# One visit per head for the 32-column products of a recurrent layer, and four output-projection tiles whose last quarter runs late

## The chip, the cores and the metric

The kernel runs on one core of a Trainium2 chip. The metric is device time in microseconds (us) of one execution. The engines are PE (matrix products; it writes PSUM), DVE (vector), ACT (scalar), POOL and SP (here: the queue that issues most DMAs).

## The reference

One inference step of two layers: layer 0 is a gated linear recurrence (HGRN2), layer 1 sliding-window attention. 272 prompt tokens (16 learned ones ahead of 256) and 64 sample tokens (8 sequences of 8) go through the same weights. Model width is 2048, layer 0 has 16 heads of 128.

```
h = x @ w_in;  q, f, i, g = split(h)          # 4 x 2048 columns
f = lb + (1 - lb) * sigmoid(f);  k = 1 - f;  v = i
per head, over time:   S <- diag(f) S + k v^T;   o = q S
o = rmsnorm(o) * norm_w * silu(g)
x <- LayerNorm(alpha * x + o @ w_out)          # then layer 1
```

The states S of the prompt and of each sample sequence are outputs too.

## The kernel before

Everything is kept transposed: channels on partitions, 336 tokens along the free axis. Weights and activations are split into a high and a low part, so that one projection product is three PE products (lines 225 to 227) with 336 columns each.

A class `Stream` (line 108) sets the order of the work. Its list `seq` names weight chunks of 4 x 128 rows; a projection tile (128 output columns) has four chunks. `run` (line 195) loads the raw weights 14 chunks ahead (`raw`, in pairs of chunks, into the pool `wraw` of four buffers, line 254), converts them 4 to 7 chunks ahead (`conv_hi` on ACT, line 159; `conv` on DVE, line 170) and issues the products. After each three products it calls `step`, which lets up to two of the side generators run (line 179). A generator says with `yield n` after how many steps it wants to go on. So a tile is 16 steps, and the yields lay every other instruction of the layer between the projections; each engine executes its own instructions in the order in which they are issued. A generator that yields too early makes PE wait, and all projections behind it.

Layer 0 runs four tiles per head in the order f, q, i, g. For each head `head_chain` (line 502) starts after tile q:

- `update` scales k and q with running products of f, at distances 1, 2, 4 (first), then 8, 16, 32, 64. The results lie in the tiles `kx`, `qx`, of which there is one set for all heads.
- First visit (lines 547 to 551): 88 products of 32 columns for the tile `lv_a` (`level`), one quarter of the array each; then, by `adv`, the tail of the head before: `psp` (three products for the prompt's state), `pss` (two for the sample states), and the three transposes of `osc` of the head before that.
- `pick` copies the wanted places of `lv_a` into a mask-selected tile `a32` (tile `a` in the profile).
- Second visit (lines 585 to 606): `lv_b` (34 products of 32 columns), `po` of the head before (28 products of 32 columns, 6 of 128), and six transposes into `pk` and `pv`.
- Behind it `at` is written from `lv_b`, `V`, `K`, `Ks`, `Vs` are copied from `pk` and `pv` in a row (lines 619 to 634), and `vm` is made on POOL.

`head_tail` (line 654) is a generator advanced by hand with `adv`: state products, their eviction and the stores of the states, `po`, the squares and `osc` (normalisation, lines 706 to 715), its transposes, and the gate with `sg`, whose result `oh`, `ol` the output projection reads. `sg` is made from tile g: a sigmoid on ACT at once, a product with PSUM on DVE two steps later (line 457).

PSUM: three banks `pj` for projection tiles, two banks `lv`, three banks `mm` for the rest. The output projection (tiles z0 to z15, line 811) needs `oh` of all heads: chunk kc reads heads 4kc to 4kc+3. So that the last heads have time, z0, z1, z2 run their chunks in turn (`kouter`, line 812). When z0 is done, the side work is drained, the pools of layer 0 are closed, and `z_chain` (line 785) evicts each z tile.

Of the kernel before, what the change touches and what calls it, by code (L numbers as in the profile page):

```python
# [21 lines left out]
F32 = mybir.dt.float32  # L22
# [7 lines left out]
P = 128  # L30
# [8 lines left out]
H = 16  # L39
# [200 lines left out]
def hybrid_trunk(tc, x_prompt, x_sample, state_hgrn, cache_k, cache_v, meta, w_in0, lb_logits, norm_w, w_out0,  # L240
# [7 lines left out]
    with es:  # L248
# [86 lines left out]
        vecs = ct("vecs", [P, P])  # L335
# [14 lines left out]
        kx, qx = [], []  # L350
        for q in range(1, 4):
            for l, nm, w in ((kx, "kx", 384), (qx, "qx", 448)):
                l.append(hp1.tile([P, w], F32, tag=f"{nm}{q}", name=f"{nm}{q}"))
                nc.gpsimd.memset(l[-1], 0.0)
# [90 lines left out]
        def epi_g(h):  # L445
            def epi(ps):
                d = head_state(h)
                sg = hp.tile([P, T], F32, tag="sg", name=f"sg{h}")
                nc.scalar.activation(sg, ps, AF.Sigmoid)
                d["sg"] = sg  # L450
                s0 = hp.tile([P, 8, P], F32, tag="s0", name=f"s0_{h}")
                nc.sync.dma_start(s0, state_hgrn[0, :, h].rearrange("b k v -> k b v"))
                d["s0"] = s0

                def chain():
                    yield 2
                    nc.vector.tensor_tensor(sg, sg, ps, op=ALU.mult)  # L457
                    ready["g", h] = True
                st.spawn(chain())
            return epi  # L460
# [5 lines left out]
        def update(k, q, m, tot, n, k2=None, q2=None, nq=None):  # L466
# [5 lines left out]
            w = min(n, 448 - (m - 1)) // (2 * m) * 2 * m  # L472
# [4 lines left out]
            if q2 is not None and not nq:  # L477
                nc.scalar.copy(halves(q2, m - 1, m, w, True), halves(q, m - 1, m, w, True))
# [4 lines left out]
        def total(h, m, tot, n):  # L483
            nb = n // (2 * m)
            o = hp.tile([P, nb], F32, tag=f"tot{2 * m}", name=f"tot{h}_{2 * m}")
# [10 lines left out]
        tails = {}  # L496

        def adv(h):
            if h in tails:
                next(tails[h], None)  # L500

        def head_chain(h):
            d = head_state(h)
            kr, qp, a32, sq, qi = d["kr"], d["qp"], d["a32"], d["sq"], d["qi"]
            at = d["at"].rearrange("p (b w) -> p b w", b=3)
            kk = [kr] + kx
            qq = [qp] + qx

            def level(pl, o, li, wide=True):
                k, q = kk[min(li, 3)], qq[min(li, 3)]  # L510
                for blk in range(3):
                    for j in range(4 if blk < 2 else 3 if wide else 1):
                        c = blk * 128 + j * 32
                        nc.tensor.matmul(pl[32 * j:32 * j + 32, o + blk * 32:o + blk * 32 + 32], k[:, c:c + 32],
                                         q[:, c:c + 32], start=True, stop=True, tile_position=(0, 32 * j),
                                         skip_group_check=True)

            def pick(pl, o, li, wide=True):
                m0 = li * 96
                r = 96 if wide else 32  # L520
                nc.vector.copy_predicated(a32[:, 0:64], mk[:, m0:m0 + 64], pl[:, o:o + 64])
                nc.vector.copy_predicated(a32[0:r, 64:96], mk[0:r, m0 + 64:m0 + 96], pl[0:r, o + 64:o + 96])

            tot = {1: d["f"]}
            yield 3
            for li in range(3):
                m = 1 << li
                update(kk[li], qq[li], m, tot[m], 352, kk[li + 1], qq[li + 1])
                tot[2 * m] = total(h, m, tot[m], 352)
                yield 4  # L530

            k8, q8 = kk[3], qq[3]
            fs = hp.tile([P, 8], F32, tag="fs", name=f"fs{h}")
            t8 = tot[8]
            nc.gpsimd.tensor_copy(fs, t8[:, 36:44])
            w64 = d["w64"]
            nc.gpsimd.tensor_copy(w64[:, 0:64].rearrange("p (b t) -> p b t", t=8)[:, :, 7], fs)

            for s in range(3):
                n = 3 if s < 2 else 2  # L540
                nc.gpsimd.tensor_tensor(sq[:, 0:96 * n].rearrange("p (j w) -> p j w", w=96)[:, :, 40 * s:40 * s + 8],
                                        q8[:, 288:288 + 24 * n].rearrange("p (j w) -> p j w", w=24)[:, :, 8 * s:8 * s + 8],
                                        w64[:, 0:24 * n].rearrange("p (j w) -> p j w", w=24)[:, :, 8 * s:8 * s + 8],
                                        op=ALU.mult)
            yield 4

            pa = lv.tile([P, 512], F32, tag="lv", name=f"lv{h}_a")
            for li in range(4):
                level(pa, 96 * li, li)
            adv(h - 1)  # L550
            adv(h - 2)
            yield 1
            update(k8, q8, 8, t8, 272)
            tot[16] = hp.tile([P, 17], F32, tag="tot16", name=f"tot{h}_16")
            t8v = t8[:, 0:34].rearrange("p (b two) -> p b two", two=2)
            nc.vector.tensor_tensor(tot[16], t8v[:, :, 0], t8v[:, :, 1], op=ALU.mult)
            for li in range(4):
                pick(pa, 96 * li, li)
            adv(h - 1)
            yield 2  # L560
            t16 = tot[16][:, 16:17]
            update(k8, q8, 16, tot[16], 256, kk[1], qq[1])
            tot[32] = total(h, 16, tot[16], 256)
            nc.vector.tensor_scalar(qq[1][:, 271:272], q8[:, 271:272], t16, None, op0=ALU.mult)
            yield 3
            adv(h - 2)
            update(kk[1], qq[1], 32, tot[32], 256, kk[2], qq[2])
            nc.scalar.copy(qi[:, 144:161], qq[1][:, 255:272])
            t64 = total(h, 32, tot[32], 256)
            t128 = hp.tile([P, 2], F32, tag="t128", name=f"t128_{h}")  # L570
            nc.vector.tensor_tensor(t128[:, 0:1], t64[:, 2:3], t64[:, 3:4], op=ALU.mult)
            yield 3
            adv(h - 1)
            k64 = kk[2]
            nc.vector.tensor_tensor(halves(kr, 0, 64, 256), halves(k64, 0, 64, 256),
                                    t64.rearrange("p (b two) -> p b two", two=2)[:, :, 1:2].to_broadcast([P, 2, 64]),
                                    op=ALU.mult)
            nc.scalar.copy(halves(kr, 0, 64, 256, True), halves(k64, 0, 64, 256, True))
            nc.vector.tensor_scalar(qi[:, 64:128], qq[2][:, 191:255], t64[:, 2:3], None, op0=ALU.mult)
            nc.scalar.copy(qi[:, 0:64], qq[2][:, 127:191])  # L580
            yield 5
            while ("i", h) not in ready:
                yield 0

            pb = lv.tile([P, 512], F32, tag="lv", name=f"lv{h}_b")
            d["pb"] = pb
            level(pb, 0, 4, wide=False)
# [11 lines left out]
            adv(h - 1)  # L599
            iT = d["iT"]  # L600
            pk = pm(f"pk{h}")
            for j in range(3):
                nc.tensor.transpose(pk[:, j * P:(j + 1) * P], (kr if j < 2 else k8)[:, j * P:(j + 1) * P], ident)
            pv = pm(f"pv{h}")
            for j in range(3):
                nc.tensor.transpose(pv[:, j * P:(j + 1) * P], iT[:, j * P:(j + 1) * P], ident)
            yield 1
            pick(pb, 0, 4, wide=False)
            for a in range(2):
                nc.scalar.copy(at[64 * a:64 * a + 32, 0:2, 64 * a + 32:64 * a + 64],  # L610
                               pb[64 * a:64 * a + 32, 96:160].rearrange("p (b w) -> p b w", b=2))
            nc.scalar.copy(at[0:64, 0:2, 64:128], pb[0:64, 160:288].rearrange("p (b w) -> p b w", b=2))
            for blk in range(3):
                o = 1 if blk < 2 else 0
                nc.vector.copy_predicated(
                    at[:, blk, o:o + 128].rearrange("p (j w) -> p j w", w=32),
                    mk[:, 480 + blk * 128:608 + blk * 128].rearrange("p (j w) -> p j w", w=32),
                    a32[:, blk * 32:blk * 32 + 32].unsqueeze(1).to_broadcast([P, 4, 32]))
# [29 lines left out]
            for w, us in ((1, (h - 1,)), (3, (h - 1,)), (6, (h,)), (2, (h - 1, h)), (1, (h - 1, h)), (4, (h,)), (3, (h,)),  # L648
                          (2, (h,)), (4, (h,)), (1, (h,))):
                yield w  # L650
                for u in us:
                    adv(u)
# [849 lines left out]
```

## Time and profile before

| | us |
|---|---|
| median of 3 runs (lowest, highest) | 1155.41 (1155.01, 1156.36) |
| the profiled execution | 1155.55 |
| its span from first to last instruction | 1153.5 |
| PE busy in the span | 1138.6 (99%) |
| DVE, ACT, POOL busy | 795.3, 619.8, 238.8 |

The 16 heads of layer 0 take from about 9 to 574 us, the output projection to about 702 us, layer 1 the rest. Lines of the timeline read: start in us, duration, engine, line of the kernel, operation, tile written <- tiles read, shapes, how many instructions are merged in the row, and in brackets the idle time ahead of it with what ended it. The durations of PE are modelled, its starts are measured. A transposition is a PE product too.

### The profile page before, as it was taken

Reading aid. Unit: us, or ns where it says so; the run is one execution under the profiler, and the core shown is the slowest. Engines: PE = TensorE matmul, PEld = TensorE weight load, DVE = VectorE, ACT = ScalarE, POOL = GpSimd, SP = SyncE. Lnnn points to the kernel's source line nnn. Section 1 sums busy time; section 2 is a strip of 40 time slices with the busy share of each in tenths; the row PEclk is TensorE's granted clock in tenths of the full one; section 3 lists DMA queues with packets and bytes.
Section 4 is the critical chain, followed back from the end, with each engine's and each line's share of the span. In section 5 each row is a group of like instructions: output and inputs, shape, how many; then the busy total and the mean of one; then the engine's idle time right before and its main releaser. Section 6 shows DMA issues by size and latency. Waiting matters only on the chain.

```text
span 1153.5 us, 26363 instructions
## 1 busy us (share of the span) xinstructions
PE 1138.6 (99%) x10151; PEld 1105.6 (96%) x10151; DVE 795.3 (69%) x2094; ACT 619.8 (54%) x1771; POOL 238.8 (21%) x343
## 2 busy tenths in 40 slices
PE   9999999999999999999999999999999999999996
PEld 9999999999999999999999999998999999999995
DVE  4766566666576565666678777577878767787657
ACT  4664555545555545555445445566666655555540
POOL 2121221212212112212134332100000011145510
PEclk9999999999999999999999999999999999999998
DMA  9654565445554545654455545653533535545572
GB/s 255 190 148 132 165 178 144 133 141 168 165 155 144 149 132 165 182 145 134 135 169 146 147 143 140 199 143 106 137 106 106 147 101 166 146 134 159 155 211 91
DMA packets 322877, 173.39 MB, mean 150 GB/s; under 512 B 19104, under 2 KB 317536, under 8 KB 322720
## 3 DMA queue, kind: packets, MB, share of 16 engines
q1 hardware_dynamic: 320656, 166.98, 51.4%
q0 software_dynamic: 1344, 4.20, 1.3%
q8 instruction: 80, 1.31, 0.5%
q10 hardware_dynamic: 752, 0.52, 0.1%
q14 instruction: 45, 0.37, 0.1%
HBM read 158.88 MB, written 14.42 MB: 150 GB/s over the span
## 4 chain that ended last, share of the span: by engine, by line
PE 94%; DVE 3%; ACT 1%; DMA 0%; issue 0%; SPq 0%; POOL 0%; DVEq 0%
PE pj_g L225 7%; PE pj_g L226 7%; PE pj_g L227 7%; PE pj_q L225 6%; PE pj_q L226 6%; PE pj_q L227 6%; PE pj_f L225 3%; PE pj_i L225 3%; PE pj_f L226 3%; PE pj_f L227 3%; PE pj_i L227 3%; PE pj_i L226 3%; PE pj_z L225 3%; PE pj_z L227 3%; PE pj_z L226 3%; PE pj_y L225 2%
## 5 line engine op out<-in xcount | busy, mean ns | idle before, releaser
L225 PE MATMUL pj_g<-xh,wlo_g 128*128 128x336 f32 (+1 forms) x512 | 163.1, 319 | 0.0
L225 PE MATMUL pj_q<-xh,wlo_q 128*128 128x336 f32 (+1 forms) x512 | 163.0, 318 | 0.0
L226 PE MATMUL pj_g<-xl,whi_g 128*128 128x336 f32 (+1 forms) x512 | 160.8, 314 | 0.0
L226 PE MATMUL pj_q<-xl,whi_q 128*128 128x336 f32 (+1 forms) x512 | 160.8, 314 | 0.0
L227 PE MATMUL pj_g<-xh,whi_g 128*128 128x336 f32 (+1 forms) x512 | 160.6, 314 | 0.0
L227 PE MATMUL pj_q<-xh,whi_q 128*128 128x336 f32 (+1 forms) x512 | 160.4, 313 | 0.0
L225 PEld LDWEIGHTS pj_q<-xh,wlo_q 128*128 128x128 f32 x512 | 96.8, 189 | 0.7
L225 PEld LDWEIGHTS pj_g<-xh,wlo_g 128*128 128x128 f32 x512 | 96.8, 189 | 0.3
L226 PEld LDWEIGHTS pj_g<-xl,whi_g 128*128 128x128 f32 x512 | 97.0, 189 | 0.0
L226 PEld LDWEIGHTS pj_q<-xl,whi_q 128*128 128x128 f32 x512 | 96.9, 189 | 0.0
L227 PEld LDWEIGHTS pj_q<-xh,whi_q 128*128 128x128 f32 x512 | 96.7, 189 | 0.0
L227 PEld LDWEIGHTS pj_g<-xh,whi_g 128*128 128x128 f32 x512 | 96.6, 189 | 0.0
L170 DVE TENSOR_TENSOR wlo_g<-raw_g,whi_g 128x512 fp32r<-128x512 f32 x128 | 91.8, 752 | 0.1
L159 ACT CAST whi_g<-raw_g 128x512 fp32r<-128x512 f32 x128 | 76.4, 622 | 21.6 <-DMA raw_g<-in_hgrn_w_in_dram 13.0
L170 DVE TENSOR_TENSOR wlo_q<-raw_q,whi_q 128x512 fp32r<-128x512 f32 x128 | 85.2, 685 | 2.5 <-ACT whi_q L159 2.5
L636 POOL TENSOR_TENSOR vm<-Vs,cst 96x512 fp32r<-96x512 f32 x32 | 33.7, 1055 | 252.4 <-DVE Vs L633 251.3
L225 PE MATMUL pj_f<-xh,wlo_f 128*128 128x336 f32 x256 | 83.2, 325 | 0.0
L225 PE MATMUL pj_z<-oh,wlo_z 128*128 128x336 f32 x256 | 81.5, 318 | 1.2 <-DVE sg L457 1.2
L225 PE MATMUL pj_i<-xh,wlo_i 128*128 128x336 f32 x256 | 81.5, 318 | 0.0
L226 PE MATMUL pj_f<-xl,whi_f 128*128 128x336 f32 x256 | 81.3, 318 | 0.0
L227 PE MATMUL pj_z<-oh,whi_z 128*128 128x336 f32 x256 | 81.3, 317 | 0.0
L227 PE MATMUL pj_f<-xh,whi_f 128*128 128x336 f32 x256 | 81.1, 317 | 0.0
(404 smaller groups left out, 3217.4 us busy)
## 6 DMA issues: line engine op xcount, KB each, us to landing
raw_z<-in_hgrn_w_out_dram SPq DMA_DIRECT2D x32, 512.0 KB
raw_q<-in_swa_w_in_dram SPq DMA_DIRECT2D x32, 512.0 KB
raw_g<-in_swa_w_in_dram SPq DMA_DIRECT2D x32, 512.0 KB
raw_f<-in_hgrn_w_in_dram SPq DMA_DIRECT2D x30, 512.0 KB
raw_q<-in_hgrn_w_in_dram SPq DMA_DIRECT2D x30, 512.0 KB
raw_i<-in_hgrn_w_in_dram SPq DMA_DIRECT2D x30, 512.0 KB
raw_g<-in_hgrn_w_in_dram SPq DMA_DIRECT2D x30, 512.0 KB
raw_y<-in_swa_w_out_dram SPq DMA_DIRECT2D x24, 512.0 KB
```

Source lines behind the costliest of these rows:

```text
L159: e.nc.scalar.copy(hi, t["raw", kc])
L170: e.nc.vector.tensor_tensor(lo, t.pop(("raw", kc)), hi.bitcast(F32), op=ALU.subtract)
L225: nc.tensor.matmul(ps, lo[:, kk, :], xh, start=first, stop=False)
L226: nc.tensor.matmul(ps, hi[:, kk, :], xl, start=False, stop=False)
L227: nc.tensor.matmul(ps, hi[:, kk, :], xh, start=False, stop=last)
L636: nc.gpsimd.tensor_tensor(vm[0:96, 4 * u:4 * u + 4, :], Vs[:, u, :].bitcast(F32).unsqueeze(1).to_broadcast([96, 4, P]), cst[0:96, 0:4].uns ...
```

## The change

1. Each head has one visit for 32-column products. `visit0(h)` issues `lv_a` of head h, then `lv_b` of head h-1 (`wide_levels`), `po` of head h-2 (`output`) and the transposes `pk`, `pv` of head h-1. After the last head two more visits finish the pipeline. A visit waits, in the order of issue, until `due(h)` says that what it reads has been issued.
2. `kx` and `qx` exist twice, by the parity of the head. `qp` and `qx` are 384 columns wide instead of 448; `sg` has three buffers, `sp` two. `nmb` and `rbc` move from the constants into a pool opened when layer 0's pools close, and `vecs` shares the buffer of `ns`.
3. `states(h)` holds what `head_tail` did for the states, as a generator of its own with its own yields: the copies of `Ks` and `Vs` stand in two groups, 13 and 18 steps behind the copies of `V` and `K`, with `vm` made in halves; `psp` and `pss` are issued 11 steps later. The last two heads have shorter pauses, `psp` ahead of the copies and in a bank `lv`.
4. `normed(h)` normalises: squares one step behind the visit, `osc` four steps later, its transposes four steps later, into a bank of their own, then the gate.
5. The tiles of a head come in the order f, q, g, i. `s0`, the sample states that are read, is loaded four steps behind the visit instead of after tile g; `sq` is made there too.
6. The output projection starts with four tiles: chunks 0 to 2 of z0, z1, z2 in turn, then chunks 0 to 2 of z3 (in a bank `lv`), then chunk 3 of all four. Their evictions are spaced by 4 steps instead of 6.

```diff
-        for nm, w in (("f", 384), ("qp", 448), ("iT", 384), ("at", 3 * 132), ("a32", 96), ("sq0", 288),
+        for nm, w in (("f", 384), ("qp", 384), ("iT", 384), ("at", 3 * 132), ("a32", 96), ("sq0", 288),
+        kx, qx = ([], []), ([], [])
+        for par in range(2):
...
-            level(pa, 96 * li, li)
+        def visit0(h, pa=None):
+            if pa is not None:
+                for li in range(4):
+                    level(hd[h], pa, 96 * li, li)
+            if 1 <= h <= H:
+                wide_levels(h - 1)
+            if h >= 2:
+                output(h - 2)
+            if 1 <= h <= H:
+                d = hd[h - 1]
+                d["pk"], d["pv"] = pm(f"pk{h - 1}"), pm(f"pv{h - 1}")
...
+            if h >= 2:
+                st.spawn(normed(h - 2), 5 if h in (H - 1, H) else 1)
+
+        def due(h):
+            return all(n < 0 or n >= H or (nm, n) in ready
+                       for nm, n in (("i", h - 1), ("b", h - 1), ("at", h - 2), ("S", h - 2),
+                                      ("Ks", h - 2)) + ((("ns", h - 2),) if h == H else ()))
...
         def head_chain(h):
...
+            while not due(h):
+                yield 0
+            pa = lv.tile([P, 512], F32, tag="lv", name=f"lv{h}_a")
+            visit0(h, pa)
+            yield 1
+            if h:
+                attended(h - 1)
+                st.spawn(states(h - 1), 2)
+                yield 1
+            for li in range(4):
+                pick(d, pa, 96 * li, li)
+            yield 2
+            update(k8, q8, 8, t8, 272)
...
+        def normed(h):
...
+            yield 4
             nc.vector.tensor_tensor(osc, po[:, 0:384].rearrange("p (j v) -> p j v", j=3),
                                     ss[:, 0:3].unsqueeze(2).to_broadcast([P, 3, P]), op=ALU.mult)
-            pt = hd[h + 1]["pb"] if h < H - 1 else pm(f"pt{h}")
+            yield 4
+            pt = pm(f"pt{h}")
...
-        first = [tiles[nm, 0] for nm in "fqig"]
+        first = [tiles[nm, 0] for nm in "fqgi"]
...
-            yield 1 + 6 * j if j < 3 else 1
+            yield 1 + 4 * j if j < 4 else 1
...
-        st.add(zt[:3], kouter=True)
-        st.add(zt[3:])
+        zt[3]["bank"] = lv, "lv"
+        for o in (st.seq, st.cseq):
+            o += [(t, kc) for kc in range(NKC - 1) for t in zt[:3]] + [(zt[3], kc) for kc in range(NKC - 1)]
+            o += [(t, NKC - 1) for t in zt[:4]]
+        st.add(zt[4:])
```

More of the change, by code (lines that the diff above doesn't have):

```diff
@@ L349, in hybrid_trunk @@
             nc.gpsimd.memset(one[nm], 1.0 if nm == "w64" else 0.0)
[L350 to L354, printed above, removed]
+        kx, qx = ([], []), ([], [])
+        for par in range(2):
+            for q in range(1, 4):
+                for l, nm, w in ((kx, "kx", 384), (qx, "qx", 384)):
+                    l[par].append(hp1.tile([P, w], F32, tag=f"{nm}{q}_{par}", name=f"{nm}{q}_{par}"))
+                    nc.gpsimd.memset(l[par][-1], 0.0)
         K2 = hp1.tile([P, P], F32, tag="K2", name="K2")
@@ L488, in total @@
             return o
[L496 to L548, printed above, removed]
-                level(pa, 96 * li, li)
[L550 to L587, printed above, removed]
@@ L608, in head_chain @@
[L608 to L618, printed above, removed]
@@ new lines, in head_chain @@
+        def head_chain(h):
+            d = head_state(h)
+            kr, qp, qi = d["kr"], d["qp"], d["qi"]
+            kk = d["kk"] = [kr] + kx[h % 2]
+            qq = d["qq"] = [qp] + qx[h % 2]
+            tot = {1: d["f"]}
+            yield 3
+            for li in range(3):
+                m = 1 << li
+                update(kk[li], qq[li], m, tot[m], 352, kk[li + 1], qq[li + 1])
+                tot[2 * m] = total(h, m, tot[m], 352)
+                yield 4
+            k8, q8, t8 = kk[3], qq[3], tot[8]
+            fs = d["fs"] = hp.tile([P, 8], F32, tag="fs", name=f"fs{h}")
+            nc.gpsimd.tensor_copy(fs, t8[:, 36:44])
+            yield 4
[12 more added lines that the diff above has]
+            update(k8, q8, 8, t8, 272)
+            tot[16] = hp.tile([P, 17], F32, tag="tot16", name=f"tot{h}_16")
+            t8v = t8[:, 0:34].rearrange("p (b two) -> p b two", two=2)
+            nc.vector.tensor_tensor(tot[16], t8v[:, :, 0], t8v[:, :, 1], op=ALU.mult)
+            s0 = d["s0"] = hp.tile([P, 8, P], F32, tag="s0", name=f"s0_{h}")
+            nc.sync.dma_start(s0, state_hgrn[0, :, h].rearrange("b k v -> k b v"))
+            w64, sq = d["w64"], d["sq"]
+            nc.gpsimd.tensor_copy(w64[:, 0:64].rearrange("p (b t) -> p b t", t=8)[:, :, 7], fs)
+            for s in range(3):
+                n = 3 if s < 2 else 2
+                nc.gpsimd.tensor_tensor(sq[:, 0:96 * n].rearrange("p (j w) -> p j w", w=96)[:, :, 40 * s:40 * s + 8],
+                                        q8[:, 288:288 + 24 * n].rearrange("p (j w) -> p j w", w=24)[:, :, 8 * s:8 * s + 8],
+                                        w64[:, 0:24 * n].rearrange("p (j w) -> p j w", w=24)[:, :, 8 * s:8 * s + 8],
+                                        op=ALU.mult)
+            yield 2
+            t16 = d["t16"] = tot[16][:, 16:17]
+            update(k8, q8, 16, tot[16], 256, kk[1], qq[1])
+            tot[32] = total(h, 16, tot[16], 256)
+            nc.vector.tensor_scalar(qq[1][:, 271:272], q8[:, 271:272], t16, None, op0=ALU.mult)
+            yield 3
+            update(kk[1], qq[1], 32, tot[32], 256, kk[2], qq[2])
+            nc.scalar.copy(qi[:, 144:161], qq[1][:, 255:272])
+            t64 = total(h, 32, tot[32], 256)
+            t128 = d["t128"] = hp.tile([P, 2], F32, tag="t128", name=f"t128_{h}")
+            nc.vector.tensor_tensor(t128[:, 0:1], t64[:, 2:3], t64[:, 3:4], op=ALU.mult)
+            yield 3
+            k64 = kk[2]
+            nc.vector.tensor_tensor(halves(kr, 0, 64, 256), halves(k64, 0, 64, 256),
+                                    t64.rearrange("p (b two) -> p b two", two=2)[:, :, 1:2].to_broadcast([P, 2, 64]),
+                                    op=ALU.mult)
+            nc.scalar.copy(halves(kr, 0, 64, 256, True), halves(k64, 0, 64, 256, True))
+            nc.vector.tensor_scalar(qi[:, 64:128], qq[2][:, 191:255], t64[:, 2:3], None, op0=ALU.mult)
+            nc.scalar.copy(qi[:, 0:64], qq[2][:, 127:191])
+            ready["b", h] = True
+            if h < H - 1:
+                return
+            while not due(H):
+                yield 0
+            yield 1
+            visit0(H)
+            yield 1
+            attended(h)
+            st.spawn(states(h), 1)
+            while not due(H + 1):
+                yield 0
+            yield 1
+            visit0(H + 1)
@@ new lines, in states, with decayed, behind_chunks, evicted @@
+        def states(h):
+            d = hd[h]
+            pk, pv, fs, s0 = d["pk"], d["pv"], d["fs"], d["s0"]
+            quick = h >= H - 2
+            V = d["V"] = hp1.tile([P, 3, P], F32, tag="V", name=f"V{h}")
+            K = hp1.tile([P, 2, P], F32, tag="K", name=f"K{h}")
+            nc.scalar.copy(V.rearrange("p j v -> p (j v)"), pv[:, 0:384])
+            nc.scalar.copy(K.rearrange("p j v -> p (j v)"), pk[:, 0:256])
+            nc.scalar.copy(K2[0:16, :], pk[0:16, 256:384])
+            Ks = hp1.tile([96, 2, P], F32R, tag="Ks", name=f"Ks{h}")
+            Vs = hp1.tile([96, 2, P], F32R, tag="Vs", name=f"Vs{h}")
+            psp, ns = [], []
+            def decayed():
+                ns.append(hp1.tile([P, 8, P], F32, tag="ns", name=f"ns{h}"))
+                nc.gpsimd.tensor_tensor(ns[0], s0, fs.unsqueeze(2).to_broadcast([P, 8, P]), op=ALU.mult)
+            def behind_chunks():
+                psp.append(lv.tile([P, 512], F32, tag="lv", name=f"psp{h}") if quick else pm(f"psp{h}"))
+                for j, (a, v) in enumerate(((K[:, 0, :], V[:, 0, :]), (K[:, 1, :], V[:, 1, :]), (K2, V[:, 2, :]))):
+                    nc.tensor.matmul(psp[0][:, j * P:(j + 1) * P], a, v, start=True, stop=True, skip_group_check=True)
+            def evicted():
+                S = d["S"] = hp1.tile([P, 2, P], F32, tag="S", name=f"S{h}")
+                nc.scalar.copy(S[:, 0, :], psp[0][:, 0:P])
+                nc.vector.scalar_tensor_tensor(S[:, 1, :], S[:, 0, :], d["t128"][:, 0:1], psp[0][:, P:2 * P],
+                                               op0=ALU.mult, op1=ALU.add)
+                sp = d["sp"] = hp1.tile([P, P], F32, tag="sp", name=f"sp{h}", bufs=2)
+                nc.vector.scalar_tensor_tensor(sp, S[:, 1, :], d["t16"], psp[0][:, 2 * P:3 * P], op0=ALU.mult,
+                                               op1=ALU.add)
+                ready["S", h] = True
+            if quick:
+                if h < H - 1:
+                    decayed()
+                yield 6
+                behind_chunks()
+                yield 2
+                evicted()
+                yield 1
+            else:
+                yield 13
+            vm = hp1.tile([P, 8, P], F32R, tag="vm", name=f"vm{h}")
+            for u in range(2):
+                r = slice(32 + 32 * u, 64 + 32 * u)
+                for t, src, again, low in ((Ks, pk, 64, 32), (Vs, pv, 32, 64)):
+                    nc.scalar.copy(t[0:32, u, :], src[r, 256:384])
+                    nc.scalar.copy(t[again:again + 32, u, :], src[r, 256:384])
+                    nc.vector.tensor_tensor(t[low:low + 32, u, :], src[r, 256:384], t[0:32, u, :].bitcast(F32),
+                                            op=ALU.subtract)
+                nc.gpsimd.tensor_tensor(vm[0:96, 4 * u:4 * u + 4, :],
+                                        Vs[:, u, :].bitcast(F32).unsqueeze(1).to_broadcast([96, 4, P]),
+                                        cst[0:96, 0:4].unsqueeze(2).to_broadcast([96, 4, P]), op=ALU.mult)
+                if u:
+                    ready["Ks", h] = True
+                yield (7 if quick else 11) if u else (3 if quick else 5)
+            if not quick:
+                behind_chunks()
+            pss = []
+            for u in range(2):
+                pss.append(pm(f"pss{h}_{u}"))
+                nc.tensor.matmul(pss[u], Ks[:, u, :], vm[0:96, 4 * u:4 * u + 4, :].rearrange("p b v -> p (b v)"),
+                                 start=True, stop=True)
+            yield 1
+            if not quick:
+                evicted()
+            if not ns:
+                decayed()
+                yield 6
+            for u in range(2):
+                nu = ns[0][:, 4 * u:4 * u + 4, :].rearrange("p b v -> p (b v)")
+                nc.vector.tensor_tensor(nu, nu, pss[u], op=ALU.add)
+            ready["ns", h] = True
+            yield 3
+            nc.sync.dma_start(st_p[0, 0, h], d["sp"])
+            nc.sync.dma_start(st_s[0, :, h].rearrange("b k v -> k b v"), ns[0])
@@ L742, in hybrid_trunk @@
         st.add(first, kouter=True)
-        st.add([tiles[nm, h] for h in range(1, H) for nm in "fqig"])
+        st.add([tiles[nm, h] for h in range(1, H) for nm in "fqgi"])
         st.raw(1, nc.scalar)
@@ L777, in epi @@
                     hes.close()
+                    lnp = nes.enter_context(tc.tile_pool(name="ln", bufs=1))
+                    for nm in ("nmb", "rbc"):
+                        LN[nm] = lnp.tile([P, T], F32, tag=nm, name=nm)
                     zp = zes.enter_context(tc.tile_pool(name="z", bufs=1))
```

162 lines of the change are left out of this document (68 added, 94 removed).

## The prediction

> **What bounds the kernel now.** I read the page first, then the chain of waits, then PE's timeline in one head of the recurrent layer and where that layer ends, and last the timelines of DVE, ACT and SP beside it.
>
> ```profile
> span 1153.5 us, 26363 instructions
> ...
> PE 94%; DVE 3%; ACT 1%; DMA 0%; issue 0%; SPq 0%; POOL 0%; DVEq 0%
> ```
>
> The chain that ended last is PE's own queue for 94% of the span. So an edit counts by what it does to the time from one PE start to the next: fewer or cheaper products, or waits of PE. Ends of products are modelled in the trace; I use starts only.
>
> ```profile
> 351.04 0.32 PE L227 MATMUL pj_g<-xh,whi_g 128*128 128x336 f32 x1
> 351.29 0.36 PE L514 MATMUL lv_a<-qp,kr 128*32 128x32 f32 x19
> 351.46 0.22 PE L514 MATMUL lv_a<-qx,kx 128*32 128x32 f32 x1
> ...
> 352.25 0.94 PE L660 MATMUL psp<-V,K 128*128 128x128 f32 x6
> ...
> 353.99 0.32 PE L226 MATMUL pj_g<-xl,whi_g 128*128 128x336 f32 x1
> ```
> ```profile
> 536.09 0.31 PE L227 MATMUL pj_f<-xh,whi_f 128*128 128x336 f32 x1
> 536.34 0.26 PE L514 MATMUL lv_b<-qx,kx 128*32 128x32 f32 x6
> ...
> 539.42 0.32 PE L226 MATMUL pj_f<-xl,whi_f 128*128 128x336 f32 x1
> ```
> ```profile
> 580.92 0.32 PE L227 MATMUL pj_z<-oh,whi_z 128*128 128x336 f32 x1
> ...
> 582.36 0.31 PE L226 MATMUL pj_z<-ol,whi_z 128*128 128x336 f32 x1
> ...
> 582.97 0.33 PE L227 MATMUL pj_z<-oh,whi_z 128*128 128x336 f32 x1
> ...
> 583.62 0.32 PE L226 MATMUL pj_z<-ol,whi_z 128*128 128x336 f32 x1
> ```
>
> Each fence runs from the last projection product ahead of an insertion to the second one behind it. From 582.36 to 582.97 stand four plain steps of one product in 0.61 us, 0.153 us each, so 0.31 us of each stretch is plain. The first visit of a head (the 88 products of `lv_a`, then `psp`, `pss` and the transposes of `osc`) costs 353.99 - 351.04 - 0.31 = 2.64 us. The second visit (`lv_b`, `po`, `pk`, `pv`) costs 539.42 - 536.09 - 0.31 = 3.02 us. The third fence shows, at the end of the layer, the same `psp` and `pss` standing alone, 582.36 - 580.92 - 0.31 = 1.13 us, and three transposes of `osc` alone, 583.62 - 582.97 - 0.31 = 0.34 us.
>
> **The visits.** The new visit is the second one with the 88 products ahead of it in the same shape, so it has no second entry and exit. Those 88 cost at most 352.25 - 351.29 = 0.96 us, with the drain before `psp`, and at least 88 x 0.17/19 = 0.79 us by the 19 from 351.29 to 351.46; I take 0.84. `psp` with `pss`, and the transposes, become insertions of their own. Per head: 2.64 + 3.02 - (3.02 + 0.84 + 1.13 + 0.34) = 0.33 us less, with 0.21 and 0.38 as ends. Fourteen heads (2 to 15) have the full visit: 14 x 0.33 = 4.6 us. The rest (heads 0 and 1, the last two visits) does the same work with one visit fewer, and `psp` and `pss` part in heads 14 and 15; I count these as nothing, with 0.3 us to either side. **Term 1: -4.6 us (-2.9 to -5.6).**
>
> The row 351.29 lies 0.25 us behind 351.04 instead of 0.153, and the step out of the 88 takes up to 0.17 us more: 0.27 us at most for entering and leaving. [...]
>
> **PE's stall at the third z tile.**
>
> ```profile
> 577.07 0.32 PE L227 MATMUL pj_z<-oh,whi_z 128*128 128x336 f32 x1
> 578.65 0.42 PE L225 MATMUL pj_z<-oh,wlo_z 128*128 128x336 f32 x1 [1.25 <-DVE sg L457]
> ```
> ```profile
> 578.09 0.50 DVE L457 TENSOR_TENSOR sg<-sg,pj_g 128x336 f32<-128x336 f32 x1
> ```
>
> z2 takes the PSUM bank of g15, and the multiplication that empties it stands on DVE behind the `Ks`/`Vs` subtractions. PE loses 578.65 - 577.07 - 0.15 = 1.43 us. In the new order i is a head's last tile; two copies on ACT empty its bank, eight steps (3.7 us) before z2 starts, and g15's multiplication comes a whole tile earlier. What would be late next is ACT, which has only the copy of S ahead of them. **Term 2: -1.4 us (0 to -1.4).** The same row gives the delay from a DVE end to PE: 578.09 + 0.50 to 578.65, 0.06 us.
>
> **A new wait: the transposes of `osc`.** Before, `osc` was ready most of a head before its transposes. Now `normed` issues them nine steps (27 projection products) behind the visit, and all projections queue behind them on PE. On DVE, in program order after the visit: two picks of `pb`, three writes of `at` (which wait for ACT's copies, and these for `po`), `ss`, eight picks of `pa`, one weight conversion, three updates, `osc`.
>
> ```profile
> 538.80 0.42 ACT L610 COPY at<-lv_b 32x64 f32<-32x64 f32 x2 [2.32 <-PE po L704]
> 539.23 0.26 ACT L612 COPY at<-lv_b 64x128 f32<-64x128 f32 x1
> ```
> ```profile
> 539.52 0.71 DVE L615 COPY_PREDICATED at<-mk,a 128x128 f32<-128x128 uint8 x3 [1.48 <-ACT at L612]
> ```
> ```profile
> 543.19 0.28 ACT L709 ACTIVATE junk<-po 128x128 f32<-128x128 f32 x1
> ```
> ```profile
> 544.39 0.17 DVE L710 TENSOR_SCALAR ss<-ss 128x3 f32<-128x3 f32 x1 [1.00 <-ACT junk L709]
> ...
> 545.89 0.56 DVE L714 TENSOR_TENSOR osc<-po,ss 128x384 f32<-128x384 f32 x1 [0.74 <-POOL ss L711]
> ```
> ```profile
> 528.29 0.30 DVE L475 TENSOR_TENSOR kx<-kx,tot 128x136 f32<-128x136 f32 x1 [5.35 <-PE lv_a L514]
> ...
> 529.83 0.34 DVE L669 SCALAR_TENSOR_TENSOR S<-S,t,psp 128x128 f32<-128x128 f32 x1
> ...
> 530.46 0.69 DVE L170 TENSOR_TENSOR wlo_f<-raw_f,whi_f 128x512 fp32r<-128x512 f32 x1
> 531.07 0.29 DVE L475 TENSOR_TENSOR kx<-kx,tot 128x128 f32<-128x128 f32 x1
> ```
>
> I count from the first `lv_b` product (536.34). ACT's `at` copies end at 539.49, +3.15. The squares follow, and `ss` starts 544.39 - 543.19 = 1.20 us behind the first of them: +4.35. It has some 0.1 us to itself (+4.45). From 528.29 to 529.83 the same three updates and eight picks took 1.54 us (+5.99), and the conversion 531.07 - 530.46 = 0.61 (+6.60). The power on POOL is no later: `osc` stood 545.89 - 544.39 = 1.50 us behind `ss`, +5.85. `osc` ends at +6.60 + 0.56 = +7.16, and PE sees it at +7.22. PE itself: its second projection product starts at 539.42, +3.08, and 26 more take 3.99 us: +7.07. So PE waits 0.15 us; with 0.1 for rounding and for the weights that cannot be fetched ahead, 0 to 0.35. It happens in the visits of heads 2 to 14, 13 times, and I take 0.12 since the sum is of whole rows that overlap a little. **Term 3: +1.6 us (0 to +4.5).**
>
> **A new wait: the raw weights of z3.** `wraw` has four buffers of two weight chunks. In the new order the chunks 2 and 3 of z0, z1 and z2 hold three of them until their last quarter is converted, which now stands behind z3's first three quarters. z3's second pair can only follow its first pair through the fourth buffer. So its load starts when DVE has converted z3's chunk 1, and the very next conversion on ACT needs it.
>
> ```profile
> 510.02 0.37 SPq L148 DMA_DIRECT2D raw_g<-in_hgrn_w_in_dram  x1
> ```
> ```profile
> 514.02 0.62 ACT L159 CAST whi_g<-raw_g 128x512 fp32r<-128x512 f32 x1 [1.24 <-DMA raw_g<-in_hgrn_w_in_dram]
> ```
>
> Issue to use is 4.0 us. I count steps (0.46 us each) from z's first product. The visit with `po` of head 14 comes at step 14: 6.4 us, plus 0.34 for the transposes of head 13 and 0.46 for `pss` of head 14 (of the 1.13 above, `psp` taking the rest) is 7.2, first product 7.3. DVE's writes of `at` end 539.52 + 0.71 - 536.34 = 3.9 us later, 11.2; the conversion of chunk 1 ends at 11.8; ACT's next one can start at 15.8 and ends at 16.4. Queued behind it on ACT are the squares of head 14, then the copy of S of head 15; behind the squares are `ss`, `osc` and PE's transposes of head 14. From first square to the end of `osc`: 545.89 + 0.56 - 543.19 = 3.26 us, so 19.7. PE arrives at step 27: 12.4 + 0.34 + 0.46 + 3.02 + 0.67 (`psp` of head 15) = 16.9. PE waits 2.8 us. It is nothing if ACT takes the squares first, and 3.5 if the load takes 0.7 us longer beside the store of the states. Head 15's output then still comes some 3 us before step 51, where z needs it. **Term 4: +2.8 us (0 to +3.5).**
>
> The rest is nothing on PE: the copies are the same, spread under steps in which ACT is idle; `s0`'s load now waits on SP for `po` two heads back, but is used a head later; the z chains come eight steps apart instead of ten, four of them, and a bank is next needed sixteen steps on. The six more memsets on POOL come at the start, ahead of any update.
>
> **Sum:** -4.6 - 1.4 + 1.6 + 2.8 = -1.6 us. The profiled execution took 1155.55 us (2.05 around its span), 0.14 above the median of the runs: 1153.9 against 1155.41. What a measurement here can tell from no change is 0.2%, 2.3 us.
>
> **The rivals.** *ACT is not held* (chance 0.24): the squares of head 14 go ahead of the conversion, or the buffer comes free otherwise. For it: the conversion stands only a step ahead of the squares. Against: four buffers, three of them taken. Time: 1153.9 - 2.8 = 1151.1, faster. *`osc` is in time, ACT is held* (0.16): DVE's instructions overlap 0.1 us more than I have it; 1152.3, faster. *Neither wait* (0.08): 1149.5. *The transposes of `osc` wait longer* (0.12), the slower side: one conversion or one ACT copy more than I count falls between `ss` and `osc`. A conversion is 0.61 us, so PE would wait 0.12 + 0.61 = 0.73 us in 13 heads, 9.5 us, and the time is 1153.9 + 7.9 = 1161.8. Beside the held ACT the point at which the whole gain is gone is (4.6 + 1.4 - 2.8) / 13 = 0.25 us per head; for it speaks that PE and `osc` are within 0.2 us of one another, against it that program order fixes what lies between. *The change does nothing to the entries* (0.02): the 88 products cost the same inside the visit as in front of `psp`, 0.96, and term 1 falls to 2.9; 1155.6.
>
> **How the numbers follow.** The forecast, both waits at the sizes above, has the remaining 0.38: 1153.9, its own range 1152.4 to 1155.6. Under 1153.1 is faster by over 0.2%: 0.24 + 0.08, 0.14 of the third case, and 0.06 of the forecast's, 0.52 in all. Within 0.2%: 0.32 of the forecast, 0.02 of the third, 0.02 of the last, and 0.02 of the longer wait where it stays small, 0.38. Slower: 0.10. The range 1149.8 to 1157.0 leaves out the longest waits (0.10) and most of the case with neither.
>
> **What would show it.** In the changed kernel's timeline: one insertion per head with `lv_a`, `lv_b`, `po`, `pk` and `pv` of about 3.86 us net, `psp` with `pss` 1.13, the transposes 0.34 plus a wait for DVE `osc`; no wait for `sg` in z; one wait for `osc` of 2 to 3 us among the first z groups, with ACT idle before it on a `raw_z` load. I am wrong if the insertions cost the same as before in sum, if PE waits for something that I have at nothing (the visit itself, `pss`, or z's last quarters for head 15), or if the raw load of z3 shows no wait.

## The result, and the profile after

The changed kernel takes 1164.29 us (median of 4 runs, 1163.25 to 1166.05) against 1155.61 beside it: 1.0076 times as long, 95% interval 1.0059 to 1.0094. It is slower, and the forecast of 1153.9 with its range to 1157.0 was wrong. The profiled execution took 1163.25 us, its span 1161.5, which is 8.0 more than before. Of the kernels in the experiments, e4 and e10 had one run each that took far longer than the others (2237 and 1866 us); no reading uses these two.

The page after, its span and the sum by engine of the chain that ended last:

```profile
span 1161.5 us, 26277 instructions
...
PE 88%; DVE 6%; ACT 2%; DMA 2%; issue 1%; POOL 1%; SPq 0%; DVEq 0%; ACTq 0%; POOLq 0%
```

PE's share fell from 94 to 88%: PE waits more. The view of PE's waits says for whom (us in total, times, longest):

```profile
engine line waited for: us in total, times, longest us
PE pj_z L225 <- DVE wlo_z L170: 4.4, 2, 3.2
PE pt L770 <- DVE osc L764: 2.6, 1, 2.6
PE pss L738 <- POOL vm L727: 1.9, 1, 1.9
PE po L558 <- DVE og L777: 1.2, 1, 1.2
```

Four kinds of waits, 10.1 us in five places, all at the head of this list and all new. `sg`, 1.25 us in the kernel before, is gone from it. First the recurrent layer, PE's timeline around the visit of one head and around its transposes:

```profile
310.29 0.32 PE L227 MATMUL pj_i<-xh,whi_i 128*128 128x336 f32 x1
310.53 0.36 PE L524 MATMUL lv_a<-qp,kr 128*32 128x32 f32 x19
...
311.37 0.20 PE L524 MATMUL lv_a<-qx,kx 128*32 128x32 f32 x1
...
314.19 0.41 PE L225 MATMUL pj_i<-xh,wlo_i 128*128 128x336 f32 x1
...
318.28 0.32 PE L227 MATMUL pj_i<-xh,whi_i 128*128 128x336 f32 x1
318.43 0.49 PE L770 MATMUL pt<-ident,osc 128*128 128x128 f32 x3
318.68 0.40 PE L225 MATMUL pj_i<-xh,wlo_i 128*128 128x336 f32 x1
```

The visit lasts from 310.29 to 314.19. The 88 products take 311.37 - 310.53 = 0.84 us, as taken in the prediction. The transposes start 0.15 us behind the product ahead of them, so nothing is waited for, and they cost 318.68 - 318.28 - 0.15 = 0.25 us. Now the output projection, PE's timeline again, one row per wait:

```profile
573.19 0.50 PE L738 MATMUL pss<-vm,Ks 96*128 96x512 f32 x1 [1.87 <-POOL vm L727]
...
587.45 0.52 PE L770 MATMUL pt<-ident,osc 128*128 128x128 f32 x3 [2.65 <-DVE osc L764]
...
590.54 0.27 PE L558 MATMUL po<-S,qi 128*32 128x128 f32 x1 [1.18 <-DVE og L777]
...
608.72 0.32 PE L227 MATMUL pj_z<-oh,whi_z 128*128 128x336 f32 x1
612.21 0.42 PE L225 MATMUL pj_z<-oh,wlo_z 128*128 128x336 f32 x1 [3.17 <-DVE wlo_z L170]
...
630.05 0.42 PE L225 MATMUL pj_z<-oh,wlo_z 128*128 128x336 f32 x1 [1.22 <-DVE wlo_z L170]
```

What stood behind each is seen on the timelines of ACT, POOL, SP and DVE, in this order:

```profile
569.26 0.47 ACT L278 CAST oh<-og 128x336 fp32r<-128x336 f32 x1 [1.45 <-DVE og L777]
...
570.59 0.26 ACT L724 CAST Vs<-pv 32x128 fp32r<-32x128 f32 x1
...
583.80 0.62 ACT L159 CAST whi_z<-raw_z 128x512 fp32r<-128x512 f32 x1 [4.77 <-DMA raw_z<-in_hgrn_w_out_dram]
```
```profile
571.60 1.54 POOL L727 TENSOR_TENSOR vm<-Vs,cst 96x512 fp32r<-96x512 f32 x1 [2.35 <-DVE Vs L725]
```
```profile
579.57 0.37 SPq L148 DMA_DIRECT2D raw_z<-in_hgrn_w_out_dram  x1
...
603.66 0.42 SPq L752 DMA_DIRECT2D out_dram<-ns  x1
```
```profile
608.67 0.50 DVE L843 SCALAR_TENSOR_TENSOR z<-xh,pj_z 128x336 f32<-128x336 f32 x1 [5.47 <-DMA out_dram<-ns]
...
611.47 1.29 DVE L170 TENSOR_TENSOR wlo_z<-raw_z,whi_z 128x512 fp32r<-128x512 f32 x2
```

`pss` of head 14 (573.19): ACT stood at the cast of head 13's output until 569.26, and the second group of copies of head 14's `Ks` and `Vs`, from which POOL makes `vm`, stood behind it. The transposes of head 14 (587.45): the wait of term 4, ACT idle 4.77 us for z3's raw weights, whose load SP could issue only at 579.57. The last visit (590.54) needs the bank that those late transposes hold. At z4 (612.21), DVE's chain of z0 waited 5.47 us to overwrite memory from which the sample states of head 15 were still being stored, and the conversion that z4 uses first stood behind it (611.47).

One more loss is no wait. Windows of PE's time (busy us and count per engine, then the granted clock):

```profile
609.47:612.88 3.41, 0.67 (x4) 0.67 (x5) 2.08 (x5) 2.09 (x4) 1.03 (x4) 1.00 0.00 0
612.88:616.29 3.41, 3.41 (x15) 3.41 (x14) 3.19 (x7) 2.44 (x5) 0.76 (x1) 0.51 0.54 156
616.29:619.70 3.41, 3.41 (x23) 3.41 (x23) 3.19 (x6) 1.40 (x4) 1.22 (x3) 0.99 0.54 154
```

After the stretch with 0.67 us of PE work the clock was granted at half for 3.41 us, and PE started 15 products instead of 23: some twelve starts follow 0.28 us apart instead of 0.153, which with the first one behind the wait is 1.6 us.

Summed over all starts of PE, the insertions of the layer and of z without those waits are 3.7 us cheaper than before, and 1.4 are gained at `sg`. The waits cost 2.8 (transposes of 14), 2.1 (`pss` of 14), 1.1 (last visit) and 4.7 (weights), each over what the same insertion costs where nothing waits. The half clock costs 1.6, and everything outside 0.7: the stretch ahead of the first visit is 0.4 shorter, and the second layer, from the end of z on, 1.1 longer. So -3.7 - 1.4 + 2.8 + 2.1 + 1.1 + 4.7 + 1.6 + 0.7 = 7.9 of the 8.0.

### The profile page after: what moved, and what is told of

Same layout as the page of the kernel before. It is cut to its first block, busy times and chain, and to the rows that moved or that the text cites. A ratio compares the mean times of both kernels' runs of the same rounds, so it can differ in the third digit from the quotient of the medians.

```text
span 1161.5 us, 26277 instructions
## 1 busy us (share of the span) xinstructions
PE 1136.4 (98%) x10151; PEld 1104.4 (95%) x10151; DVE 833.8 (72%) x2094; ACT 615.5 (53%) x1771; POOL 258.3 (22%) x349
## 4 chain that ended last, share of the span: by engine, by line
PE 88%; DVE 6%; ACT 2%; DMA 2%; issue 1%; POOL 1%; SPq 0%; DVEq 0%; ACTq 0%; POOLq 0%
PE pj_g L225 7%; PE pj_g L226 7%; PE pj_g L227 7%; PE pj_q L225 6%; PE pj_q L226 6%; PE pj_q L227 6%; PE pj_i L225 3%; PE pj_f L225 3%; PE pj_i L227 3%; PE pj_f L226 3%; PE pj_i L226 3%; PE pj_f L227 3%; PE pj_y L226 2%; PE pj_y L227 2%; PE pj_y L225 2%; PE pj_z L225 2%
## 5 line engine op out<-in xcount | busy, mean ns | idle before, releaser
L170 DVE TENSOR_TENSOR wlo_g<-raw_g,whi_g 128x512 fp32r<-128x512 f32 x128 | 128.8, 1040 | 0.4
L225 PE MATMUL pj_i<-xh,wlo_i 128*128 128x336 f32 x256 | 84.0, 328 | 0.0
L226 PE MATMUL pj_z<-ol,whi_z 128*128 128x336 f32 x256 | 81.7, 319 | 0.0
L227 PE MATMUL pj_i<-xh,whi_i 128*128 128x336 f32 x256 | 81.0, 316 | 0.0
```

The lines of the kernel that those rows point to most:

```text
L170: e.nc.vector.tensor_tensor(lo, t.pop(("raw", kc)), hi.bitcast(F32), op=ALU.subtract)
L225: nc.tensor.matmul(ps, lo[:, kk, :], xh, start=first, stop=False)
L226: nc.tensor.matmul(ps, hi[:, kk, :], xl, start=False, stop=False)
L227: nc.tensor.matmul(ps, hi[:, kk, :], xh, start=False, stop=last)
```

## The experiments

**The order of the raw weights, and the store.** My theory after the result: term 4 was right and is paid as forecast, the three others I had missed, and the wait at z4 is the store's. Four kernels follow, each beside the kernel before (1155.67 us); behind each time stand its ratio to the kernel before and the 95% interval. e1 undoes the order written out by hand:

```
-            o += [(t, kc) for kc in range(NKC - 1) for t in zt[:3]] + [(zt[3], kc) for kc in range(NKC - 1)]
-            o += [(t, NKC - 1) for t in zt[:4]]
+        st.add(zt[:4], kouter=True)
```

> The changed kernel, but z0 to z3 run all four chunks in turn, so the second pairs of raw weights need no fifth buffer. Theory (every wait in the output projection has a cause of its own; the 2.8 us at the transposes of head 14 and the 1.3 us at the last visit come from the raw load of z3): both waits go, about 4.1 us off 1164.3, so 1160.2; the 3.3 us wait for converted weights behind z3 stays. Rival (the last heads are late as a whole, and a wait that is removed is handed on to the next one): 1163 to 1164.5, with the next wait longer by as much.

1159.65 us, 1.0034 [1.0022, 1.0047]. Its waits of PE:

```profile
PE pj_z L225 <- DVE wlo_z L170: 4.3, 2, 2.8
PE pss L738 <- POOL vm L727: 1.9, 1, 1.9
```

The wait for `osc` is gone, that of the last visit shrinks to 0.2, and 4.6 us are gained (3.7 by the spans of the two profiles). Term 4's mechanism is shown.

e2 keeps the changed kernel and leaves out one store:

```
-            nc.sync.dma_start(st_s[0, :, h].rearrange("b k v -> k b v"), ns[0])
+            if h < H - 1:
+                nc.sync.dma_start(st_s[0, :, h].rearrange("b k v -> k b v"), ns[0])
```

> The changed kernel without the store of head 15's sample states (that part of the output is left out). Theory (DVE waits 5.5 us for that store before it can write the first z tile into the freed pool, PE runs out of converted weights for 3.3 us, and the slow clock behind that idle time costs 1.5): 4.8 us off, so 1159.5, with all products behind the wait at 0.153 us. Rival (handed on): 1163 to 1164.5. Rival (the slow clock has another cause): the products at 0.28 us stay, 1161.

1162.94 us, 1.0060 [1.0047, 1.0074]: 1.4 less, where I had said about 5. Its waits:

```profile
PE pj_z L225 <- DVE wlo_z L170: 4.0, 3, 1.7
...
```

The waits at z4 (3.2) and z6 (1.2) became three, at z4, z5 and z6. The half clock did not go either: it now follows the wait of `pss`, from 574.5. My theory fell here: the store was only the last to arrive, and something else makes the weights late.

e3 is both edits together:

> Both edits at once: z0 to z3 in turn, and the store of head 15's sample states left out. Theory (causes are independent): 8.9 us off, 1155.4, the time of the kernel before. Rival (handed on): above 1159.

1159.16 us, 1.0028 [1.0017, 1.0039]: 0.5 less than e1. The store is worth next to nothing.

**The gate of head 13.** e4 is e1 with the output of head 13 held back three steps more, behind the copies of head 14:

```
-                st.spawn(normed(h - 2), 5 if h in (H - 1, H) else 1)
+                st.spawn(normed(h - 2), 8 if h == H - 1 else 5 if h == H else 1)
```

> z0 to z3 in turn, and the normalisation of head 13 starts 8 steps behind its visit instead of 5, so that its cast of the gated output no longer stands on ACT ahead of the second group of Ks and Vs copies of head 14. Theory (those copies make POOL and then the state products of head 14 late by 2.1 us): 2.1 us less than with z0 to z3 in turn alone, so about 1158.1. Rival (POOL or the copies are late for another reason, for instance the freeing of pk and pv): the state products still wait about 2 us, 1160.2.

1156.22 us, 1.0002 [0.9993, 1.0011]: 3.4 less than e1. The same kernel ran again, as e8, for a profile:

> The kernel of e4 once more, for a profile of it. Theory: 1156.2 us; no wait of pss of head 14 for vm (2.1 us in e1), and, since there is no idle stretch of 2 us or more there, nothing else new; 1.3 us of the 3.4 that e4 gained over e1 must lie in another wait that became shorter. Rival: the wait for vm is only half as long, and the rest lies in the products' rate: products of 0.28 us are gone behind z4's start.

1156.17 us. The wait for `vm` is gone. That is 2.1 us; the rest is 1.6 for the half clock, which no longer appears, and 0.6 of the weights' waits, less 0.6 for a last visit that now waits longer: 2.1 + 1.6 + 0.6 - 0.6 = 3.7 against 3.4 measured. Both the theory and the rival had a part of it.

**The order in which a tile uses its weights.** In the kernel, z4 and later tiles use their last quarter first, while the conversions run in the order of the quarters. So a tile starts with what is converted last. e5 changes this in e4's kernel:

```
-        st.add(zt[4:])
+        st.add(zt[4:], last_first=False)
```

> The kernel of e4 (1156.2 us), and z4 to z15 use their weight quarters in the order of conversion instead of the last one first. Theory: the waits for converted weights at the start of a z tile come from the order, since the quarter that the tile uses first is the one converted last, so that it stands on VectorE behind the chains of z0 to z3. In e1's profile these are 2.9 us at z4, 1.8 at z6 and 1.5 of slow products behind the first: 1150 to 1151. Rival: VectorE is short of time in this stretch whatever the order, and the same waits come one to three quarters later: 1155 to 1156.2.

1151.67 us, 0.9970 [0.9960, 0.9981]: 4.5 less than e4, and faster than the kernel before. DVE's timeline in e8, then e8's PE:

```profile
604.13 1.28 DVE L170 TENSOR_TENSOR wlo_z<-raw_z,whi_z 128x512 fp32r<-128x512 f32 x2
```
```profile
603.79 0.32 PE L227 MATMUL pj_z<-oh,whi_z 128*128 128x336 f32 x1
604.87 0.42 PE L225 MATMUL pj_z<-oh,wlo_z 128*128 128x336 f32 x1 [0.76 <-DVE wlo_z L170]
```

The same two in e5, and the head of its view of waits:

```profile
596.03 1.89 DVE L170 TENSOR_TENSOR wlo_z<-raw_z,whi_z 128x512 fp32r<-128x512 f32 x3
...
604.11 1.29 DVE L170 TENSOR_TENSOR wlo_z<-raw_z,whi_z 128x512 fp32r<-128x512 f32 x2
```
```profile
603.58 0.32 PE L227 MATMUL pj_z<-oh,whi_z 128*128 128x336 f32 x1
603.74 0.31 PE L225 MATMUL pj_z<-oh,wlo_z 128*128 128x336 f32 x1
...
609.30 0.32 PE L225 MATMUL pj_z<-oh,wlo_z 128*128 128x336 f32 x1
```
```profile
PE pw L319 <- DVE mhalf L274: 1.1, 1, 1.1
```

DVE converts z4's last quarter at the same time in both, 604.13 and 604.11. In e8 PE needs it at once and waits. In e5 it starts z4 at 603.74 with the first quarter, converted from 596.03 on, and reaches the last one at 609.30. No wait in z is left; the longest of the whole run is one in the prologue that the kernel before has too. DVE was not short of time; its work was used in the wrong order.

e6 spreads the chains in e4's kernel and keeps the order of use:

```
-            yield 1 + 4 * j if j < 4 else 1
+            yield 1 + 6 * j if j < 4 else 1
```

> The kernel of e4 (1156.2 us), and the chains of z0 to z3 start 1, 7, 13 and 19 steps behind their tiles instead of 1, 5, 9 and 13. Theory: the conversion of z4's last quarter stands on VectorE behind fewer chains, and those of z5 and z6 too, since the chains are spread over more steps: 1 to 4 us less, 1152 to 1155. Rival: what VectorE waits for is the buffer of the chain of z2 and the store ahead of it, and the spacing only moves that wait: 1156 to 1157.

1156.83 us, 1.0010 [1.0001, 1.0019]: no gain. The waits for weights are 3.3 us in two places instead of 3.5 in three. Moving chains moves the wait; the rival holds.

e9 puts e5's line, and nothing else, into the changed kernel:

> The changed kernel (1164.3 us) with z4 to z15 using their weight quarters in the order of conversion, and nothing else changed. Theory: in the changed kernel's profile the waits at the starts of z4 and z6 (3.3 and 1.4 us) and the 12 slow products behind the first (1.6) come from the order of use alone, since VectorE converts at the same times in e5 and e8: 6.3 us less, 1158.0; the waits of pss of head 14, of the transposes of head 14 and of the last visit stay. Rival: here the chains of z0 to z3 start later than in e5, behind the store of head 15's states, so that the first quarters of z4 are late as well: 1160 to 1163.

1158.98 us, 1.0034 [1.0020, 1.0047]: 5.3 less than the changed kernel, where 6.3 was expected. PE's waits:

```profile
PE pt L770 <- DVE osc L764: 2.9, 1, 2.9
PE pss L738 <- POOL vm L727: 1.9, 1, 1.9
...
PE pj_z L225 <- DVE wlo_z L170: 0.7, 1, 0.7
```

4.4 us of waits for weights became 0.7. The half clock did not go, it moved: it now follows the wait of `pss` (below).

e10 puts it into the kernel before, as a control:

```
-        st.add(zt[3:])
+        st.add(zt[3:], last_first=False)
```

> The kernel before (1155.6 us) with z3 to z15 using their weight quarters in the order of conversion. Theory: no wait of TensorE for converted weights stands in its z tiles, so the order is worth nothing there, and what e5 gains on the kernel before is the visits' and sg's: 1155.2 to 1156.0. Rival: the order is a gain by itself, as in e5 against e4: 1151 to 1154.5.

1156.00 us, 1.0002 [0.9993, 1.0011]. The order of use is worth nothing there, since PE arrives at z4 after its last quarter is converted: in the kernel before DVE starts that conversion at 604.73, and PE reaches z4 at 608.36. So e5's gain of 0.3% on the kernel before is not the order's own; it is what the visits and `sg` bring when nothing in z eats it.

**The order of a head's tiles.** e7 is e1 with f, q, i, g (and the same order where the first head's tiles are listed):

```
-            for nm, off, epi in (("f", 1, epi_f), ("q", 0, epi_q), ("g", 3, epi_g), ("i", 2, epi_i)):
+            for nm, off, epi in (("f", 1, epi_f), ("q", 0, epi_q), ("i", 2, epi_i), ("g", 3, epi_g)):
...
-        st.add([tiles[nm, h] for h in range(1, H) for nm in "fqgi"])
+        st.add([tiles[nm, h] for h in range(1, H) for nm in "fqig"])
```

> The kernel of e1 (1159.65 us), and the four tiles of a head come in the order f, q, i, g as in the kernel before, so that z2 takes the bank of g15 again. Theory of term 2: the wait for the multiplication of sg comes back, 1.4 us at z2's first product: 1160.7 to 1161.4. Rival: the subtractions of Ks and Vs no longer stand ahead of that multiplication, and the order of the tiles is worth nothing: 1159.4 to 1160.0.

1161.44 us, 1.0051 [1.0038, 1.0063], 1.8 more than e1. `iT` is held once for all heads; with i a tile earlier, a visit transposes the next head's values. The instructions are the same in kind and number.

```profile
572.55 0.42 PE L225 MATMUL pj_z<-oh,wlo_z 128*128 128x336 f32 x1 [2.34 <-DVE sg L456]
```

The wait for `sg` comes back. It is longer than 1.4, while the wait of `pss` behind it is shorter (0.5 more than plain, for 2.1) and seven products at half clock follow: the total agrees with term 2, its parts overlap with others.

**The half clock.** e11 makes PE wait in a place of its own. In e5's kernel the conversion of the first quarter of z9, z12 and z15 is written several times over:

```
-            e.nc.vector.tensor_tensor(lo, t.pop(("raw", kc)), hi.bitcast(F32), op=ALU.subtract)
+            raw = t.pop(("raw", kc))
+            for _ in range({"z9_0": 14, "z12_0": 16, "z15_0": 14}.get(f"{t['name']}_{kc}", 1)):
+                e.nc.vector.tensor_tensor(lo, raw, hi.bitcast(F32), op=ALU.subtract)
```

> The kernel of e5, in which VectorE writes the low part of the first weight quarter of z9, z12 and z15 14, 16 and 14 times over instead of once (same values), so that TensorE has to wait there: some 2.3 us at z9, 3 to 5 at z12 and 2 to 4 at z15, worked out from e5's distance between conversion and use. Theory: after a wait of 2.9 us or more the next 12 or so products start 0.28 us apart instead of 0.153, and after one below 2.5 us they do not; some 8 to 14 us more than e5 in all. Rival: the slow products belong to the place, not to the wait, and none appear here.

1170.33 us in one run, 18.7 more than e5 where 8 to 14 were expected: the gaps at z9 and z15 and the slow stretches came out longer than planned. From one product's start to the next there were 3.60 us at z9, 3.42 at z12 and 4.48 at z15. Windows of e11, with their edges within 0.1 us of the changes of the clock:

```profile
640.20:643.61 3.41, 0.98 (x7) 0.70 (x5) 3.27 (x5) 0.00 (x0) 0.00 (x0) 1.00 0.00 0
643.61:647.02 3.41, 2.56 (x9) 2.56 (x10) 3.27 (x7) 0.94 (x2) 0.00 (x0) 0.51 0.13 35
647.02:650.44 3.42, 3.42 (x14) 3.42 (x13) 3.30 (x6) 2.61 (x6) 2.54 (x3) 0.50 0.40 118
...
667.50:670.91 3.41, 2.17 (x15) 1.89 (x13) 3.24 (x6) 0.00 (x0) 0.00 (x0) 1.00 0.00 0
670.91:674.33 3.42, 1.55 (x10) 1.55 (x11) 3.28 (x7) 0.01 (x1) 0.00 (x0) 1.00 0.00 0
```

Neither theory nor rival holds as written. The slow products do follow the wait, but not by its length: 3.60 us at z9 gave two slow windows (20 products), 3.42 at z12 none. The slow stretch at z9 begins at 643.7, the one behind z15 ends at 705.1: 61.4 us, 18 times 3.41. In e7 two slow stretches begin at 573.0 and 610.5, 11 times 3.41 apart. So in each of these two runs the slow stretches lie on a grid of 3.41 us, and at z12 of e11 the idle time fell into two of its windows, 2.17 and 1.55 us busy. In e9, at `pss`, a gap of only 2.3 us fell into one:

```profile
570.07:573.48 3.41, 1.54 (x9) 1.15 (x8) 3.32 (x6) 2.20 (x6) 1.54 (x1) 1.00 0.40 109
573.48:576.90 3.42, 3.42 (x51) 3.06 (x53) 1.89 (x4) 0.10 (x1) 0.00 (x0) 0.51 0.00 0
```

## Why the prediction was wrong, step by step

**Term 1** was right for what it counted. By the medians of all visits, a full head costs 3.76 + 1.14 + 0.25 = 5.15 us of insertions instead of 2.54 + 2.93 = 5.47: 0.32 less, where I had 0.33. The 14 heads bring 4.5; some visits took longer than their median, by 1.3 us in sum, and the first and last heads, counted at nothing, bring some 0.5. That leaves -3.7, inside the bounds. (The upper bound should have been -2.6: the 0.3 for the other heads was added at one end alone.)

**Term 2** was right: -1.4, and e7 brings the wait back.

**Term 3** was wrong by its whole size, 1.6: behind none of the visits of heads 2 to 14 do the transposes wait. In the head shown above PE reaches them 318.43 - 311.37 = 7.06 us behind the first `lv_b` product, as counted (7.07). What was mis-sized is the step from the squares to `ss`. ACT's timeline in the kernel before, then ACT's and DVE's in the changed one:

```profile
543.59 0.28 ACT L709 ACTIVATE junk<-po 128x128 f32<-128x128 f32 x1
```
```profile
314.41 0.27 ACT L760 ACTIVATE osc<-po 128x128 f32<-128x128 f32 x1
...
314.67 0.26 ACT L760 ACTIVATE osc<-po 128x128 f32<-128x128 f32 x1
```
```profile
315.31 0.17 DVE L761 TENSOR_SCALAR ss<-ss 128x3 f32<-128x3 f32 x1
...
317.53 0.54 DVE L764 TENSOR_TENSOR osc<-po,ss 128x384 f32<-128x384 f32 x1
```

Before, the three squares write one tile, `junk`, and start 0.40 us apart (543.19, 543.59). In the changed kernel each writes its own part of `osc`, and they start 0.26 apart. So `ss` starts 0.90 us behind the first square where I took 1.20 from the old row, and the squares start 0.11 earlier: +3.94 instead of +4.35. From there to `osc` were 2.22 us, against 2.25 counted. `osc` ends at 318.07, 0.36 us ahead of its transposes. That the shared tile is what sets the 0.40 is my estimate from these rows; no run tested it alone.

**Term 4** was right in mechanism, place and size: 2.8 us forecast, 2.8 over plain measured, the row at 587.45 showing 2.65 as waiting. Counted from z's first product (565.51), PE was ready at +19.1 and `osc` at +21.8, where I had 16.9 and 19.7: the wait of `pss` ahead of both moved both, and the difference held. e1 takes the wait away.

**What failed is the sentence "The rest is nothing on PE"**, and within it two claims. "The copies are the same, spread under steps in which ACT is idle": for head 14 ACT was not idle, it stood at the cast of head 13's output, and `pss` waited, 2.1 us (e4, e8). "The z chains come eight steps apart instead of ten, four of them, and a bank is next needed sixteen steps on": I looked at who needs the chains' banks, and not at what stands behind the chains on DVE. There stand the conversions for z4 to z6, and a z tile uses the last of its four first. In the kernel before, PE has z3's four quarters between the first chains and z4, and the conversion is in time (e10). In the new order z0 to z3 end together just ahead of z4, and 4.7 us are lost (e5, e9). The last visit's 1.1 is a follower of term 4, which I ended at the transposes without asking who waits for their bank. The half clock's 1.6, behind the window with 0.67 us of PE work (609.47), was in no term. These four, 9.5 us, with the 0.9 that term 1 fell short and the 0.7 outside, less term 3's 1.6, are the 9.5 us between the forecast of -1.6 and the 7.9 found in the trace.

I had named such waits among the marks of error ("if PE waits for something that I have at nothing") and given it no price and no chance; my slower rival was another mechanism. A list of what is queued behind each moved step on its own engine, as I made for ACT in term 4, would have shown the conversions behind the chains.

With those waits removed, e5 gains 3.7 us by the spans against the 6.0 of terms 1 and 2. Its longer visits explain 1.9 of the 2.3 that is missing. Prologue and second layer together are 0.8 slower, less 0.5 that the first and last heads bring; why the second layer is slower is open.

## What to carry to other kernels

When tiles are reordered, follow every queue that feeds the next tile, not only the queues of the moved tile: here the matmul order was right and the converted weights for the tile behind it came late. Use data in the order in which it is produced; "last first" costs three quarters of a tile of lead (603.74 to 609.30 in e5), and stays hidden until something delays the producer. When removing what a wait names leaves the sum of waits as it was (e2), the named one only came last; look for what orders the queue.

## What the runs showed of the hardware

Every figure here is read from the profiles of the runs above.

The clock. In the changed kernel it was granted at half for 3.41 us behind the wait at z4, and the products started 0.28 us apart instead of 0.153. From the start of e11's first slow stretch to the end of its last are 18 times 3.41 us, and between the starts of e7's two 11 times, so I counted PE's work in windows of a grid of that length. Half clock followed a window with 0.67 us of it in the changed kernel, 0.98 in e11 and 1.54 in e9; with 1.55, at z12 of e11, it did not; and with 2.56 us busy at half clock a second slow window followed (643.61). These windows begin up to 0.1 us early. With the edges exactly at the changes of the clock, the windows at full clock ahead of a slow one held 0.58 (e7 from 607.11, e11 from 694.88), 0.76 (the changed kernel from 609.56), 1.14 (e1 from 606.10) and 1.53 to 1.55 us of PE work (e2, e3, e9, from 570.15 to 571.10; its ends are modelled). Windows with 1.62 us (e11 from 670.99, the changed kernel from 585.66), 1.75 (e1 from 571.96) and 2.23 (the changed kernel from 572.01) were followed by full clock. The length of the gap did not decide it: one of 2.3 us was enough in e9, and one of 3.42 us was not in e11. What sets the clock was not shown.

The visit of the ninth full head took 4.74 us from the projection product ahead of it (380.00) to the one behind it (384.74) in the changed kernel, 0.83 longer than the median visit with 3.91. Most of it lies between two rows of `po`, 382.24 and 383.05, of which 0.39 us are idle with PE waiting for nothing that the profile shows; e5 has the same place (383.20 to 383.99, 0.36 idle). No experiment was made on it.
